# Score products of the first block's windowed attention: from three products on 64 rows to two on 128

## The chip, the cores and the metric

The kernel runs on one core of a Trainium2 chip. Its time is the device time of one execution in microseconds (us). Five engines work side by side: TensorE (PE in the profile, its weight loads PEld), VectorE (DVE), ScalarE (ACT), GpSimd (POOL) and SyncE (SP), which here issues nearly all DMAs. Each engine executes its own instructions in the order in which they stand.

## The reference

Two transformer blocks run over 512 tokens of 1024 features, all in float32. The change concerns the scores of the first block's windowed attention: 16 query heads of 64 features, four key heads (each for four query heads), query blocks of 128 tokens, each against the keys of its own block and of the two neighbours.

```python
def windowed_gqa_sink(q, k, v, sink):
    ...
    s = jnp.einsum('bnqgrd,bnkgd->bngrqk', qb, kw).astype(jnp.float32) * (d ** -0.5) + bias[None]
    sink_f = sink.astype(jnp.float32).reshape(1, 1, kvh, r, 1, 1)
    m = jnp.maximum(jnp.max(s, axis=-1, keepdims=True), sink_f)
    p = jnp.exp(s - m)
    denom = jnp.sum(p, axis=-1, keepdims=True) + jnp.exp(sink_f - m)
    o = jnp.einsum('bngrqk,bnkgd->bnqgrd', (p / denom).astype(v.dtype), vw)
```

The same normed input also feeds a state-space branch (SSD, eight groups) and two gates. After that come cross attention and a feed-forward part, and then the second block with its mixture of experts.

## The kernel before

**Precision.** TensorE multiplies operands of type fp32r, which hold fewer bits than float32. So every float32 operand of a dense product is split into a rounded part ("hi", or h) and the rest ("lo", or l), and a product becomes three: hi·hi, hi·lo and lo·hi (`mm3`, lines 275 to 279; the trace names lines 277, 278 and 279 for them). A weight unit of 128x1024 numbers is loaded by a DMA (`load_w`, line 266), rounded by ACT (`wh`, line 269) and completed by DVE (`wl`, line 272).

**Order of block 1** (`block1`). The input is normed, transposed and split into `hTh` and `hTl`. `attn_in` makes keys and values, `dt_section` the SSD's step sizes, `attention` the windowed attention, and `ssd` the SSD groups, with the gates (`gates1`) and the attention's output projection (`branch_a`) put among them. The program is written in this order. A scheduler in the tile framework then sets the order on each engine, by the dependencies and by its own estimates of durations, so that dense products of `ssd_in` and `gates1` (in the trace `mm<-hTh,wh` and the like) stand between the steps of the attention heads. No table in the kernel sets this.

**Keys.** `attn_in` projects 256 key features in two tiles of 128 rows, two key heads on top of each other. `kn` keeps each tile as it is and a second time with its halves swapped: one ACT copy of 128 rows (line 456), then two DMAs that move 64 rows each (lines 457 and 458). Four splits give `kh` and `kl`. Thus each key head lies once on rows 0 to 63 and once on rows 64 to 127.

**Queries.** Eight projections of 128 features give two query heads each, the first on rows 0 to 63, the second on rows 64 to 127. ACT writes the rounded part, scaled by 1/8, to `atH` (line 480), DVE the rest to `atL` (line 481), 128 rows at a time.

**Heads.** For each pair of heads, each head and each query block b, a score tile `sc` of 128 x L is made, where L is 256 for the first and the last block and 384 for the others. It is `mm3` with 64 rows of query and of key: the weights are the query block (64x128), the moving operand the keys (64xL). That makes 16 x 4 tiles and 192 products. DVE adds the alibi term and takes the maximum (line 508), and the four maxima of a head are negated (line 511). ACT exponentiates the sink's term (line 512) and each tile (line 515), and PE transposes the tile (`pt`, line 520). ACT or DVE copies it out (lines 523 and 525), and PE multiplies it with the values (`o`, line 528). After a pair of heads DVE divides (line 535), PE transposes the result (`ot`, line 540), and its split takes the place of the pair's queries in `atH` and `atL`. `sc`, `pt`, `o` and `ot` share three PSUM banks.

**What follows.** `ssd_p1` of a group works on four chunks. A chunk needs two broadcast loads `cs<-csd` (line 728), POOL's step matrices `D` (lines 696 and 698), a DVE chain (lines 732, 735 and 736) and then PE's products `yd` (line 741). `branch_a` begins when the last head's result is split: its products read `mm<-atH,wh` in the trace, and DVE closes each of its eight units with line 624 (`ta`).

Of the kernel before, what the change touches and what calls it, by code (L numbers as in the profile page):

```python
# [9 lines left out]
F32 = mybir.dt.float32  # L10
# [4 lines left out]
OP = mybir.AluOpType  # L15
# [11 lines left out]
def _units_b(w, cols):  # L27
    """Column blocks of 128 with all of K: [unit, partition, K tile, 128]."""
    K = w.shape[0]
    kt = K // 128  # L30
    return np.ascontiguousarray(
        np.stack([w[:, c].reshape(kt, 128, 128).transpose(1, 0, 2) for c in cols]))
# [6 lines left out]
def host_arrays(inp):  # L39
# [6 lines left out]
    def units_a(w, C=256, kt=4):  # L46
        """[column block, K half, partition, kt, C]"""
        K, N = w.shape
        return np.ascontiguousarray(
            w.reshape(K // (128 * kt), kt, 128, N // C, C).transpose(3, 0, 2, 1, 4))  # L50
# [117 lines left out]
class Emit:  # L168
# [30 lines left out]
    def psum(self, stack, n, mm, sa, sm):  # L199
        """the eight banks: dense products, two kinds of chains"""  # L200
# [30 lines left out]
    # ---------------------------------------------------------------- tools  # L231
# [49 lines left out]
    def proj_b(self, ps, units, act, halves=False):  # L281
        """feature-major: ps[128 cols, n tok]; units: list of W along K; act(k) -> (hi, lo)
        halves: the first half of the tokens as soon as it is there"""
# [19 lines left out]
    def proj_a(self, banks, units, act):  # L303
        """token-major: banks: psum tiles, two token tiles of 256 columns each; act(k, t) -> (hi, lo)"""
# [11 lines left out]
    def split(self, hi, lo, src, scale=None):  # L316
        """hi + lo = src * scale (scale: per-partition AP or None)"""
# [11 lines left out]
    def rstd(self, out, ss, n, eps=EPS):  # L329
        """out = (ss / n + eps) ** -0.5"""  # L330
# [5 lines left out]
    def rsqrt(self, v, eps, scale=1.0, tile=None):  # L336
        """(scale * v + eps) ** -0.5: a first guess from the bits, then Newton's iteration"""
# [13 lines left out]
    def norm_out(self):  # L351
        """where normed rows go, transposed and split: put(t, h, x) takes half a tile; hT(k) -> (hi, lo)"""
# [14 lines left out]
    def norm_T(self, gname):  # L367
        """rmsnorm of token-major tiles, transposed and split: step(t, x) takes a tile"""
# [80 lines left out]
    def attn_in(self):  # L449
        nc, a = self.nc, self.a  # L450
        # keys: natural and half-swapped, split
        kn = self.A("kn", (128, 2, 2, 512), F32)
        for m in range(2):
            ps = self.PM()
            self.proj_b(ps, [self.w0 if m == 0 else self.wb(8 + m)], self.hB, True)
            nc.scalar.copy(kn[:, 0, m, :], ps)
            nc.sync.dma_start(kn[0:64, 1, m, :], kn[64:128, 0, m, :])
            nc.sync.dma_start(kn[64:128, 1, m, :], kn[0:64, 0, m, :])
        self.kh = self.A("kh", (128, 2, 2, 512))
        self.kl = self.A("kl", (128, 2, 2, 512))  # L460
        for s in range(2):
            for m in range(2):
                self.split(self.kh[:, s, m, :], self.kl[:, s, m, :], kn[:, s, m, :])
# [7 lines left out]
    def attention(self):  # L471
        nc, a = self.nc, self.a
        # the result of a tile of queries takes the place of the queries
        self.atH = [self.A("atH") for _ in range(2)]
        self.atL = [self.A("atL") for _ in range(2)]
        for i in range(8):
            ps = self.PM()
            self.proj_b(ps, [self.wb(i)], self.hB)
            qh, ql = self.atH[i // 4][:, i % 4, :], self.atL[i // 4][:, i % 4, :]
            nc.scalar.activation(qh, ps, AF.Copy, scale=0.125)  # L480
            nc.vector.scalar_tensor_tensor(ql, ps, 0.125, qh.bitcast(F32), op0=OP.mult, op1=OP.subtract)
        for i in range(8):
            qh, ql = self.atH[i // 4][:, i % 4, :], self.atL[i // 4][:, i % 4, :]
# [4 lines left out]
            for hf in range(2):  # L488
# [3 lines left out]
                pr = slice(64 * hf, 64 * hf + 64)  # L492
                sw = 0 if hf == n % 2 else 1
                kh, kl = self.kh[pr, sw, n // 2, :], self.kl[pr, sw, n // 2, :]
# [5 lines left out]
                for b in range(4):  # L500
# [5 lines left out]
                    self.mm3(sc[:, :L], qh[pr, qs], ql[pr, qs], kh[:, k0:k1], kl[:, k0:k1], True, True)  # L506
# [95 lines left out]
    def gates1(self, f0, f1):  # L602
        """tanh of the halved gates, feature-major, to DRAM"""
# [10 lines left out]
    def branch_a(self):  # L614
        """(1 + tanh(ga / 2)) * (attn @ Wa), feature-major, to DRAM"""
# [11 lines left out]
    def conv(self, ps, ct, ntap, first, silu_scale=True):  # L627
        """half of the centred depthwise convolution of a psum tile, then 2 * half * sigmoid = silu"""
# [15 lines left out]
    def ssd_in(self, g):  # L644
        """projections of group g: B, C, x (feature-major, convolved) and the doubled silu of z (token-major)"""
# [18 lines left out]
    def ssd_p1(self, g, inp):  # L664
        """the part inside the chunks, and the chunks' states"""
# [4 lines left out]
        # token-major x and B  # L670
# [19 lines left out]
        # D[s, l]: the step of the forward direction for l >= s and that of the backward one for l <= s  # L690
# [10 lines left out]
        # per chunk: the part inside the chunk, and the chunk's states  # L701
# [5 lines left out]
        for c in range(4):  # L707
# [11 lines left out]
            # raw states into the slot that they feed: forward c + 1, backward c - 1  # L719
# [26 lines left out]
    def ssd_p2(self, g, st, yh, yl, j0):  # L746
        """the states' part, gate, norm, transposition"""
# [29 lines left out]
        # y carries a factor of 2 from the doubled silu: its mean square and the guard carry 4  # L777
# [4 lines left out]
    def ssd_p3(self, g, st, yh, yl, j0):  # L782
        """the normed rows, transposed"""
# [51 lines left out]
    def branch_b(self, p, yh, yl):  # L835
        """ssd @ Wb, a quarter of K at a time; the last quarter merges the branches"""
# [29 lines left out]
    def add_units(self, xs, src, nk, act, scale=1.0, last=True, then=None):  # L866
        """xs += scale * (act @ w), w as [column block, K part, ...] of 256 columns;
        last: the last columns go token tile by token tile; then(): the step that takes them"""
# [34 lines left out]
    def then(self, gname):  # L903
        """norm_T, begun when it is called; its results in nB"""
# [5 lines left out]
    def cross_mem(self):  # L910
        """the memory, normed and transposed"""
# [143 lines left out]
    def last_norm(self):  # L1055
        """the norm at the end of the first block and the first of the second: with s, q the mean squares of x and of x g,
        x <- x g (s + eps) ** -0.5, and of that the norm: x g (q + eps (s + eps)) ** -0.5 times its gain"""
# [1254 lines left out]
```

## Time and profile before

| what | value |
|---|---|
| time, three runs | 2176.49, 2178.56 (median), 2189.05 us |
| profiled execution | span 2182.1 us from the first to the last instruction |
| busy in the span | PE 93%, PEld 79%, DVE 62%, ACT 41%, POOL 23% |
| score products | first at 97.2 us, last at 287.9 us |

The profile gives no time of its own for that execution beside the span. Its span lies 3.5 us above the median of the three runs and within them. Times in rows count from the span's first instruction. A matmul's end is modelled, and successive matmuls overlap, so what a product costs PE in a stream is the distance from its start to the next start. "Granted clock" is a share of TensorE's full clock of 2.4 GHz; 0.50 is 1.2 GHz.

### The profile page before, as it was taken

The numbers are of one execution on the slowest core, as the hardware profiler recorded it, in microseconds if no ns is written. First come the engines' busy times: TensorE is split into PE (matmuls) and PEld (weight loads), VectorE is DVE, ScalarE is ACT, GpSimd is POOL, SyncE is SP. The second block draws the span as 40 slices with busy tenths as digits, with TensorE's granted clock in tenths as the row PEclk, the third lists the DMA queues.
The fourth block names the chain that finished last, engine by engine and source line by source line (L and its number), as shares of the span: only waits on it lengthen the run. The fifth ranks groups of instructions, "written<-read, shape, count | busy, mean of one in ns | idle before, by whom it ended". The sixth has DMA issues, their size and how long they took to land. (4 is left out here: it accounts for less than half of the span.)

```text
span 2182.1 us, 31237 instructions
## 1 busy us (share of the span) xinstructions
PE 2033.9 (93%) x11818; PEld 1730.2 (79%) x11818; DVE 1362.7 (62%) x2622; ACT 892.3 (41%) x1630; POOL 504.9 (23%) x515
## 2 busy tenths in 40 slices
PE   7999988989999988999999999899899999998995
PEld 7788877877787777888999999787878768886774
DVE  4566446786978765466334444667789452538885
ACT  4344434444545343254323222542232333246773
POOL 0000034034433142101111101503511110224444
PEclk9999999999999999999999999998899899998997
DMA  4211234323333254422222223224212104677976
GB/s 168 84 67 63 78 101 159 116 72 112 94 107 100 88 157 157 156 88 69 97 97 96 88 97 116 97 79 122 91 50 76 45 21 158 223 296 245 324 269 165
DMA packets 131302, 266.71 MB, mean 122 GB/s; under 512 B 22256, under 2 KB 67696, under 8 KB 127050
## 3 DMA queue, kind: packets, MB, share of 16 engines
q1 hardware_dynamic: 127690, 256.26, 35.5%
q0 software_dynamic: 3456, 8.39, 1.7%
q8 instruction: 95, 1.56, 0.3%
q14 instruction: 61, 0.50, 0.1%
HBM read 242.93 MB, written 25.35 MB: 123 GB/s over the span
## 5 line engine op out<-in xcount | busy, mean ns | idle before, releaser
L272 DVE TENSOR_TENSOR wl<-wr,wh 128x1024 fp32r<-128x1024 f32 (+1 forms) x272 | 316.4, 1164 | 288.9 <-ACT wh L269 277.9
L269 ACT CAST wh<-wr 128x1024 fp32r<-128x1024 f32 (+1 forms) x272 | 264.5, 973 | 548.5 <-PE mm L278 282.8
L279 PE MATMUL mm<-hTh,wl 128*128 128x512 f32 (+1 forms) x1056 | 412.4, 391 | 1.3 <-DVE wl L272 1.3
L277 PE MATMUL mm<-hTh,wh 128*128 128x512 f32 (+1 forms) x1056 | 411.9, 390 | 1.6 <-ACT hTh L320 0.9
L278 PE MATMUL mm<-hTl,wh 128*128 128x512 f32 (+1 forms) x1056 | 410.7, 389 | 0.8 <-DVE hTl L321 0.8
L279 PEld LDWEIGHTS mm<-hTh,wl 128*128 128x128 f32 x1056 | 203.4, 193 | 42.4 <-issue 5.1
L277 PEld LDWEIGHTS mm<-hTh,wh 128*128 128x128 f32 x1056 | 203.2, 193 | 39.6 <-issue 2.6
L278 PEld LDWEIGHTS mm<-hTl,wh 128*128 128x128 f32 x1056 | 203.2, 192 | 39.2 <-issue 3.2
L710 POOL TENSOR_TENSOR xw<-xt,dtT 128x256 f32<-128x256 f32 (+1 forms) x32 | 29.8, 932 | 551.4 <-ACT xt L678 551.4
L278 PE MATMUL mm<-wl,hTh 128*128 128x256 f32 x512 | 150.1, 293 | 0.0
L277 PE MATMUL mm<-wh,hTh 128*128 128x256 f32 x512 | 149.8, 293 | 0.0
L279 PE MATMUL mm<-wh,hTl 128*128 128x256 f32 x512 | 149.3, 292 | 0.0
L278 PE MATMUL mm<-wl,uh 128*128 128x256 f32 x512 | 145.0, 283 | 0.0
L279 PE MATMUL mm<-wh,ul 128*128 128x256 f32 x512 | 144.8, 283 | 0.0
L277 PE MATMUL mm<-wh,uh 128*128 128x256 f32 x512 | 144.7, 283 | 0.0
L876 DVE SCALAR_TENSOR_TENSOR x<-mm,x 128x256 f32<-128x256 f32 x152 | 57.5, 420 | 93.4 <-PE mm L279 92.8
L1042 POOL TENSOR_TENSOR ul<-r,uh 128x512 fp32r<-128x512 f32 x32 | 41.7, 1303 | 274.8 <-ACT uh L1041 274.8
L278 PEld LDWEIGHTS mm<-wl,hTh 128*128 128x128 f32 x512 | 100.9, 197 | 1.7 <-issue 0.7
L277 PEld LDWEIGHTS mm<-wh,hTh 128*128 128x128 f32 x512 | 100.8, 197 | 1.0 <-issue 0.2
L279 PEld LDWEIGHTS mm<-wh,hTl 128*128 128x128 f32 x512 | 100.8, 197 | 0.7 <-issue 0.5
L278 PEld LDWEIGHTS mm<-wl,uh 128*128 128x128 f32 x512 | 98.2, 192 | 0.5 <-DVE wl L272 0.2
L277 PEld LDWEIGHTS mm<-wh,uh 128*128 128x128 f32 x512 | 98.2, 192 | 0.3
(571 smaller groups left out, 4706.2 us busy)
## 6 DMA issues: line engine op xcount, KB each, us to landing
mr<-in_w_egu_dram SPq DMA_DIRECT2D x32, 1024.0 KB, 8.4
wr<-in_win_b_dram SPq DMA_DIRECT2D x59, 512.0 KB, 3.3
cs<-csd SPq DMA_DIRECT2D x64, 256.0 KB, 4.5
wr<-in_w_up_dram SPq DMA_DIRECT2D x32, 512.0 KB, 3.3
wr<-in_w_down_dram SPq DMA_DIRECT2D x32, 512.0 KB, 3.3
wr<-in_w_ed_dram SPq DMA_DIRECT2D x32, 512.0 KB, 4.5
wr<-in_w_b_dram SPq DMA_DIRECT2D x29, 512.0 KB, 3.3
wr<-in_win_a_dram SPq DMA_DIRECT2D x18, 512.0 KB, 3.3
```

Of the source, the lines that this page charges most:

```text
L269: nc.scalar.copy(w.hi, raw)
L272: e.tensor_tensor(w.lo, raw, w.hi.bitcast(F32), op=OP.subtract)
L277: mm(out, lh, rh, start=start, stop=False, skip_group_check=skip)
L278: mm(out, lh, rl, start=False, stop=False, skip_group_check=skip)
L279: mm(out, ll, rh, start=False, stop=stop, skip_group_check=skip)
L710: nc.gpsimd.tensor_tensor(xw[:, d0:d1], h3(xt[c])[:, None].to_broadcast([128, d1 - d0, 4, 64]), self.dtdec[:, c, d0:d1, H][:, :, :, None]. ...
L876: nc.vector.scalar_tensor_tensor(xv, ps[t // 2][:, (t % 2) * 256:(t % 2 + 1) * 256], scale, xv, op0=OP.mult, op1=OP.add)
L1042: nc.gpsimd.tensor_tensor(ul[:, j, :], r, uh[:, j, :].bitcast(F32), op=OP.subtract)
```

## The change

Each query head's rounded part and rest are stacked: head 0 of a pair has its rounded part on rows 0 to 63 and its rest on rows 64 to 127 of `atH`; head 1 has its rounded part on rows 64 to 127 and its rest on rows 0 to 63 of `atL`. For that ACT and DVE work on 64 rows at a time, and DVE writes to the other half of the rows from that which it reads. `kn` holds, for each key head, the same 64 features on both halves. A score tile is then the stack against `kh` plus the stack against `kl`, two products on 128 rows, which also contain the term lo·lo. The diff also takes out docstrings and comments, and later line numbers shift by two.

```diff
     def attn_in(self):
...
         kn = self.A("kn", (128, 2, 2, 512), F32)
+        h0, h1 = slice(0, 64), slice(64, 128)
         for m in range(2):
             ps = self.PM()
             self.proj_b(ps, [self.w0 if m == 0 else self.wb(8 + m)], self.hB, True)
-            nc.scalar.copy(kn[:, 0, m, :], ps)
-            nc.sync.dma_start(kn[0:64, 1, m, :], kn[64:128, 0, m, :])
-            nc.sync.dma_start(kn[64:128, 1, m, :], kn[0:64, 0, m, :])
+            for e, (own, other) in enumerate(((h0, h1), (h1, h0))):
+                nc.scalar.copy(kn[own, m, e, :], ps[own])
+                nc.sync.dma_start(kn[other, m, e, :], kn[own, m, e, :])
...
-        for s in range(2):
-            for m in range(2):
-                self.split(self.kh[:, s, m, :], self.kl[:, s, m, :], kn[:, s, m, :])
+        for m in range(2):
+            for e in range(2):
+                self.split(self.kh[:, m, e, :], self.kl[:, m, e, :], kn[:, m, e, :])
...
     def attention(self):
...
-            qh, ql = self.atH[i // 4][:, i % 4, :], self.atL[i // 4][:, i % 4, :]
-            nc.scalar.activation(qh, ps, AF.Copy, scale=0.125)
-            nc.vector.scalar_tensor_tensor(ql, ps, 0.125, qh.bitcast(F32), op0=OP.mult, op1=OP.subtract)
+            for q, own, other in ((self.atH, slice(0, 64), slice(64, 128)), (self.atL, slice(64, 128), slice(0, 64))):
+                q = q[i // 4][:, i % 4, :]
+                nc.scalar.activation(q[own], ps[own], AF.Copy, scale=0.125)
+                nc.vector.scalar_tensor_tensor(q[other], ps[own], 0.125, q[own].bitcast(F32), op0=OP.mult, op1=OP.subtract)
...
-                pr = slice(64 * hf, 64 * hf + 64)
-                sw = 0 if hf == n % 2 else 1
-                kh, kl = self.kh[pr, sw, n // 2, :], self.kl[pr, sw, n // 2, :]
+                q = (self.atL if hf else self.atH)[i // 4][:, i % 4, :]
+                kh, kl = self.kh[:, n // 2, n % 2, :], self.kl[:, n // 2, n % 2, :]
...
-                    self.mm3(sc[:, :L], qh[pr, qs], ql[pr, qs], kh[:, k0:k1], kl[:, k0:k1], True, True)
+                    nc.tensor.matmul(sc[:, :L], q[:, qs], kh[:, k0:k1], start=True, stop=False)
+                    nc.tensor.matmul(sc[:, :L], q[:, qs], kl[:, k0:k1], start=False, stop=True)
```

The scheduler also sets another order, from `dt_section` up to about the projections for the SSD's third group; from there on PE's order is that of before. Three places follow. The first is PE behind the second pair of heads (`ot` is that pair's result, `sc` the scores of the next head, `mm` dense products), before:

```order
653 L540 MATMUL ot<-consts,o 128x128 x4
654 L277 MATMUL sc<-kh,atH 128x256
655 L278 MATMUL sc<-kl,atH 128x256
656 L279 MATMUL sc<-kh,atL 128x256
657 L277 MATMUL sc<-kh,atH 128x384
658 L278 MATMUL sc<-kl,atH 128x384
659 L279 MATMUL sc<-kh,atL 128x384
660 L279 MATMUL mm<-wh,hTl 128x256
```

and now:

```order
652 L542 MATMUL ot<-consts,o 128x128 x4
653 L507 MATMUL sc<-kh,atH 128x256
654 L508 MATMUL sc<-kl,atH 128x256
655 L507 MATMUL sc<-kh,atH 128x384
656 L508 MATMUL sc<-kl,atH 128x384
657 L279 MATMUL mm<-wh,hTl 128x256
```

The third product of each tile is gone, and dense products stand around the score tiles as before. The second place is DVE in `dt_section`, among the first query splits (`dtx` is what PE's transposes wait for), before:

```order
31 L1153 RECIPROCAL dtu<-dtu 64x512
32 L481 SCALAR_TENSOR_TENSOR atL<-mm,atH 128x512
33 L1154 TENSOR_TENSOR dte<-dte,dtu 64x512
34 L272 TENSOR_TENSOR wl<-wr,wh 128x1024
35 L1155 TENSOR_TENSOR dtl<-dtl,dte 64x512
36 L1156 SCALAR_TENSOR_TENSOR dtx<-dtx,dtl 64x512
```

and now:

```order
31 L1155 RECIPROCAL dtu<-dtu 64x512
32 L484 SCALAR_TENSOR_TENSOR atH<-mm,atH 64x512
33 L1156 TENSOR_TENSOR dte<-dte,dtu 64x512
34 L272 TENSOR_TENSOR wl<-wr,wh 128x1024
35 L1157 TENSOR_TENSOR dtl<-dtl,dte 64x512
36 L484 SCALAR_TENSOR_TENSOR atL<-mm,atL 64x512
37 L1158 SCALAR_TENSOR_TENSOR dtx<-dtx,dtl 64x512
```

One query split more stands ahead of `dtx`. The third place is DVE in the first chunk of the SSD's first group, behind the last head (`cs` is the chain that PE's `yd` waits for, `ta` closes a unit of `branch_a`), before:

```order
332 L732 SCALAR_TENSOR_TENSOR cs<-cs,dtT 128x128 x4
333 L272 TENSOR_TENSOR wl<-wr,wh 128x1024
334 L735 TENSOR_TENSOR cs<-cs,CB 128x512
335 L736 TENSOR_TENSOR cs<-cs,D 128x512
336 L743 TENSOR_TENSOR y<-yd,sk 128x256
```

and now:

```order
345 L734 SCALAR_TENSOR_TENSOR cs<-cs,dtT 128x128 x4
346 L626 SCALAR_TENSOR_TENSOR ta<-ta,mm 128x512
347 L272 TENSOR_TENSOR wl<-wr,wh 128x1024
348 L737 TENSOR_TENSOR cs<-cs,CB 128x512
349 L738 TENSOR_TENSOR cs<-cs,D 128x512
350 L745 TENSOR_TENSOR y<-yd,sk 128x256
```

A unit of `branch_a` is closed inside the chain, because the dense products of the gates, which stood here before, are used up among the heads now: behind the last `ot` 49 of them were left before, and 1 is left now.

## Rows read from the trace of the kernel before

**Rows 1.** The page's part 1: busy time, share of the span, instructions
```profile
PE 2033.9 (93%) x11818; PEld 1730.2 (79%) x11818; DVE 1362.7 (62%) x2622; ACT 892.3 (41%) x1630; POOL 504.9 (23%) x515
```

**Rows 2.** Windows: busy us and instructions of each engine, granted clock, DMA
```profile
97.00:298.00 201.00, 200.99 (x1236) 168.73 (x1235) 115.63 (x278) 90.20 (x228) 0.00 (x0) 1.00 0.21 69
...
310.00:315.00 5.00, 0.89 (x4) 0.39 (x3) 4.90 (x5) 0.63 (x1) 4.92 (x5) 0.81 0.15 28
315.00:325.00 10.00, 8.45 (x27) 7.14 (x28) 4.73 (x10) 3.35 (x8) 6.32 (x7) 0.58 0.39 125
...
400.00:420.00 20.00, 19.97 (x115) 17.32 (x114) 16.90 (x24) 7.69 (x10) 0.00 (x0) 1.00 0.30 105
```

**Rows 3.** Tile sc: the third product, count, min/median/max ns, first and last start, forms
```profile
L279 PE MATMUL sc<-kh,atL x64: 274/307/342, 97.5 to 288.0; 64*128 64x256 f32 x32, 64*128 64x384 f32 x32
```

**Rows 4.** Timeline of PE around two score tiles: start, duration, instruction
```profile
186.28 0.39 PE L277 MATMUL mm<-hTh,wh 128*128 128x512 f32 x1
186.50 0.39 PE L278 MATMUL mm<-hTl,wh 128*128 128x512 f32 x1
186.82 0.44 PE L277 MATMUL sc<-kh,atH 64*128 64x384 f32 x1
187.10 0.33 PE L278 MATMUL sc<-kl,atH 64*128 64x384 f32 x1
187.28 0.33 PE L279 MATMUL sc<-kh,atL 64*128 64x384 f32 x1
187.45 0.28 PE L277 MATMUL sc<-kh,atH 64*128 64x256 f32 x1
187.57 0.28 PE L278 MATMUL sc<-kl,atH 64*128 64x256 f32 x1
187.69 0.28 PE L279 MATMUL sc<-kh,atL 64*128 64x256 f32 x1
187.89 0.50 PE L279 MATMUL mm<-hTh,wl 128*128 128x512 f32 x1
188.23 0.40 PE L277 MATMUL mm<-hTh,wh 128*128 128x512 f32 x1
188.47 0.39 PE L278 MATMUL mm<-hTl,wh 128*128 128x512 f32 x1
```

**Rows 5.** Timeline of PE: the first product of the first and of the last run
```profile
97.16 0.38 PE L277 MATMUL sc<-kh,atH 64*128 64x256 f32 x1
...
287.12 0.44 PE L277 MATMUL sc<-kh,atH 64*128 64x384 f32 x1
```

**Rows 6.** Tiles kn and atH: count, min/median/max ns, first and last start, forms
```profile
L456 ACT COPY kn<-mm x2: 582/585/588, 27.4 to 31.6; 128x512 f32<-128x512 f32 x2
...
L480 ACT ACTIVATE atH<-mm x8: 588/590/592, 54.8 to 98.0; 128x512 fp32r<-128x512 f32 x8
L481 DVE SCALAR_TENSOR_TENSOR atL<-mm,atH x8: 620/684/691, 56.6 to 99.4; 128x512 fp32r<-128x512 f32 x8
```

**Rows 7.** Timelines of DVE and of PE in dt_section
```profile
59.60 0.68 DVE L1156 SCALAR_TENSOR_TENSOR dtx<-dtx,dtl 64x512 f32<-64x512 f32 x1
...
60.34 0.27 PE L581 MATMUL p<-consts,dtx 64*128 64x64 f32 x1 [0.64 <-DVE dtx L1156]
```

**Rows 8.** Waits from 97 to 298 us: total us, times, longest
```profile
PEld o L528 <- ACT pT L523: 1.9, 9, 0.3
PEld sc L277 <- DVE m L508: 1.8, 5, 0.4
...
PEld o L528 <- DVE pT L525: 1.6, 7, 0.3
```

**Rows 9.** Waits of PE from 300 to 420 us: total us, times, longest
```profile
PE yd L741 <- DVE cs L736: 12.0, 5, 5.7
```

**Rows 10.** Timeline of PE behind the heads, and line L624 of DVE
```profile
316.56 1.94 PE L741 MATMUL yd<-xt,cs 128*128 128x64 f32 x8 [5.66 <-DVE cs L736]
318.25 0.77 PE L279 MATMUL mm<-hTh,wl 128*128 128x512 f32 x1
...
L624 DVE SCALAR_TENSOR_TENSOR ta<-ta,mm x8: 670/680/689, 328.2 to 390.6; 128x512 f32<-128x512 f32 x8
```

More of the change, by code (lines that the diff above doesn't have):

```diff
@@ L478, in attention @@
             self.proj_b(ps, [self.wb(i)], self.hB)
-            qh, ql = self.atH[i // 4][:, i % 4, :], self.atL[i // 4][:, i % 4, :]
-            nc.scalar.activation(qh, ps, AF.Copy, scale=0.125)
-            nc.vector.scalar_tensor_tensor(ql, ps, 0.125, qh.bitcast(F32), op0=OP.mult, op1=OP.subtract)
+            for q, own, other in ((self.atH, slice(0, 64), slice(64, 128)), (self.atL, slice(64, 128), slice(0, 64))):
+                q = q[i // 4][:, i % 4, :]
+                nc.scalar.activation(q[own], ps[own], AF.Copy, scale=0.125)
+                nc.vector.scalar_tensor_tensor(q[other], ps[own], 0.125, q[own].bitcast(F32), op0=OP.mult, op1=OP.subtract)
         for i in range(8):
-            qh, ql = self.atH[i // 4][:, i % 4, :], self.atL[i // 4][:, i % 4, :]
             n = i // 2
```

## Prediction, on record before the changed kernel ran

> **What bounds the kernel now.** I read the page's busy shares first, then windows over the stage that the change touches, then the timeline of PE inside that stage, and last the waits. The page shows PE busy for 93% of the span, far ahead of DVE [rows 1], so the question is whether PE also bounds the heads. From 97 to 298 us it is busy for 200.99 of 201 us at a granted clock of 1.00, while DVE is busy for 115.6 us and ACT for 90.2 us [rows 2]. Busy is not yet streaming, because ends of matmuls are modelled. So I looked at starts. Dense 512-column products follow each other every 0.22 to 0.24 us, and 384-column and 256-column score products every 0.17 to 0.18 and 0.12 us, but around each run of score products four distances are longer [rows 4]. The stage is bound by PE's stream and by those longer distances, and the weight loads of `o` and `sc` wait only 5.3 us in all for ACT and DVE [rows 8], hidden behind running products. Behind the heads it is different: from 310 to 315 us PE works 0.89 of 5 us, and the clock falls to 0.81 and then 0.58 [rows 2], because `yd` waits 5.66 us for DVE [rows 10]. From 300 to 420 us there are five such waits, 12.0 us together [rows 9].
>
> **The third product.** 64 products disappear, 32 of 256 columns and 32 of 384 [rows 3]. In the stream a 256-column one costs 0.12 us and a 384-column one 0.175 us, the mean of 0.18 and 0.17 [rows 4]: 32 x 0.12 + 32 x 0.175 = 3.8 + 5.6 = 9.4 us. The two that remain read 128 rows instead of 64. I take their cost as unchanged: the 128-row dense products show that PE sustains 512 columns in 0.23 us, the same 0.45 ns a column as the 0.175 us for 384 [rows 4].
>
> **The distances around a run.** With 0.23 us for a dense product, the last dense product before the run costs 0.32 us (186.50 to 186.82), 0.09 too much. The first score product costs 0.28 instead of 0.175, 0.105 too much. The last one costs 0.20 instead of 0.12, 0.08 too much, and the dense product behind it 0.34, 0.11 too much; the next is 0.01 late [rows 4]. That is 0.40 us for each run, whatever its length. In the timeline I count 40 runs of score products, the first from 97.16 and the last from 287.12 us [rows 5], so 40 x 0.40 = 16.0 us. A score product on 64 rows next to a dense one on 128 is what these places share, and afterwards no such neighbours are left. How much of the 16.0 us goes is not shown before: nothing of it, if the cost belongs to the score tiles and not to their rows, or all of it. I take all, because within a run and within the dense stream no distance is long, only where the two meet [rows 4].
>
> The Trainium skill, page "TensorEngine Tiling (Array Packing)", section "Key Properties", says that changing the tiling mode, and not just the tile, drains TensorE. By that rule the 40 changes into 64 rows and back are the cause and all 16.0 us go; without it only the 9.4 us would be sure. It gives no price; the rows do, 0.40 us for both changes of a run.
>
> Together 9.4 + 16.0 = 25.4 us come off PE's stream.
>
> **What is added on ACT and DVE.** The query parts take 16 ACT and 16 DVE instructions instead of 8 and 8. A DVE step of 64x512 takes 0.68 us [rows 7], as long as the query split of 128x512, 0.684 us [rows 6]; so halving the rows saves nothing, and 8 x 0.59 = 4.7 us of ACT and 8 x 0.68 = 5.5 us of DVE are added. Writing to the other half of the rows isn't shown in this trace. I take the same 0.68 us; half of it or twice would be the ends. A projection keeps PE busy for 24 x 0.23 = 5.5 us, and its splits (2 x 0.59 us of ACT, 2 x 0.68 us of DVE) fit beside it, so I cost them at nothing; with that cover gone they would cost up to 5.5 us. The exception is `dt_section`: PE already waits 0.64 us for `dtx` [rows 7], and one split more stands ahead of it. It costs 0.68 us, and two more dense products (0.46 us) now stand ahead of PE's wait, so 0.2 us are lost, 0 to 0.7 as bounds. The keys need four ACT copies instead of two, 2 x 0.585 us more [rows 6], still four DMAs, and the later splits wait for all of them. ACT's next weight cast stands behind that, but `kh` is first read at 97.16 us [rows 5], some 60 us later. I cost it at nothing, 1.2 us at most.
>
> **What the new order gives back among the heads.** Ahead of the last head's result 48 more dense products are spent, 48 x 0.23 = 11 us of work that merely moves. So the heads should shorten by 25.4 - 11 = 14 us, from 12.5 us (200 us for 16) to 11.6 us each. Within that time each head's chain (maximum on DVE, exponentials on ACT, transposes, copies) must still fit. Its weight loads already start as the producer ends [rows 8]. Where a run of score products lies between producer and consumer, PE arrives about 0.2 us earlier than now (half of the 0.40). At three such places in each of 16 heads that would be 9.6 us; with the added dense products as cover it can be 0. I take 2 us, near the low end, since all waits together in rows 8 are 5.3 us and hidden.
>
> **What it gives back behind the heads.** The first SSD chunk now has `ta`, 0.68 us [rows 10], inside the DVE chain that `yd` waits for, and in the second group the convolution steps of the next projections come forward among its chunks. The dense products between the first and the last `yd` of both groups stay about the same in number (291 before, 287 now, counted in the two orders). So the 12.0 us of waits remain and grow somewhat. Bounds: 4 us less, if one of the shorter waits closes, and 12 us more, if all double. I take 2.5 us, near the 0.68 us for each of four chunks.
>
> **The sum.** 25.4 - 0.2 - 2 - 2.5 = 20.7 us. Against the profiled execution that makes a span of 2182.1 - 20.7 = 2161.4 us. That span lies 3.5 us above the median of the three runs, and no other part of the execution is shown; from the median the time is 2178.6 - 20.7 = 2158 us. Everything after about 420 us stands in the same order and is fed by short prefetches, so an earlier start should carry to the end.
>
> **Rivals.**
> - *Nothing is given back.* The heads' added fillers cover each chain, and the SSD waits do not grow. PE's 19.97 busy of 20 us from 400 to 420 us [rows 2] speaks for a stage that takes in what comes; the just-in-time weight loads [rows 8] speak against. 2178.6 - 25.4 = 2153 us.
> - *The change doesn't free the switches.* If the long distances belong to score tiles and not to 64 rows, they stay, and there are 51 runs in the new order instead of 40: 9.4 - 11 x 0.40 = 5.0 us gained, 2174 us. That each run pays once, whatever its length, speaks against it.
> - *The chains take over.* The heads lose 9.6 us, or the SSD waits double (12 us): 2178.6 - 25.4 + 12 = 2165 us, and up to 2169 with part of both. For it: five `yd` waits already [rows 9]. Against: the new order puts about as many dense products behind each head's scores as before, and their times among the heads are covered today [rows 2].
> - *Slower: the SSD chunks stall as the first one does.* Place: `yd` in the two first groups. The first such wait costs 5.7 us and then work at the lower of the two clocks, 1.2 GHz for part of the time: from 315 to 325 us the mean is 0.58, so (1 - 0.58) x 8.45 busy us = 3.5 us, 9.2 us in all [rows 2, 10]. If DVE, loaded with the convolution steps, made four more of the eight chunks wait so, 36.8 us would be lost against 25.4 won: 2190 us. It decides from three such waits on. Against it: DVE is busy for only 4.73 of the 10 us from 315 to 325 [rows 2].
>
> **How the numbers follow.** The forecast, 2158 us, has a chance of 0.60; its own range is 2153 to 2164 (0 to 10 us given back). Nothing given back: 0.15. Switches stay: 0.07. Chains take over: 0.13. Slower: 0.05. The range from 2150 us (all 25.4 us and about 3 us less of `yd` waits) to 2172 us (most of the chains' case) leaves out about 2 in 10. About 1%, 21.8 us or a time under 2156.8, is what a measurement can tell from no change. Of the forecast's 0.60 about 0.24 lies there, and of the first rival 0.14: 0.38 for faster. Slower by over 1% needs more than 2200 us, 0.02 out of the last rival. The rest, 0.60, is within 1%.
>
> **What would show it.** Right: two products for each of 64 tiles on 128 rows; dense products beside them at 0.23 us, with no distance of 0.32 or 0.34; the last run of score products at about 275 us (12 us earlier) and about 20 us gained at 420 us and at the end. Wrong: a granted clock below 1.00 among the heads, weight loads that leave PE idle there for more than 5 us, `yd` waits of over 18 us in the two groups, query splits much longer than 0.68 us, or long distances that remain around score tiles.

## The result, and the profile after

The changed kernel takes 2161.78 us, the median of 8 runs (2152.91 to 2170.14). The kernel before, run beside it on the same chip, takes 2183.94 us (8 runs, 2171.73 to 2189.05). The ratio is 0.9899, with a 95% interval from 0.9872 to 0.9926: about 22 us or 1.0% less, and the interval reaches to both sides of 1%. The forecast was 20.7 us less, 2158 us. Its 2158 stood on the median of three runs of the kernel before, 2178.56 us; the eight runs lie 5.4 us higher, so the differences are what can be compared.

The page's part 1 of the kernel after, beside [rows 1]: PE has 64 instructions less, DVE 8 and ACT 10 more.

```profile
PE 2000.5 (93%) x11754; PEld 1711.1 (80%) x11754; DVE 1367.0 (64%) x2630; ACT 898.7 (42%) x1640; POOL 503.8 (23%) x515
```

**The score products.** The tile view of `sc` in the kernel after: line, engine, operation, count, shortest/median/longest ns, first and last start, forms. Each of the 64 tiles is made by two products, on 128 rows.

```profile
L507 PE MATMUL sc<-kh,atH x32: 274/338/446, 98.3 to 266.1; 128*128 128x256 f32 x16, 128*128 128x384 f32 x16
L508 PE MATMUL sc<-kl,atH x32: 278/308/340, 98.4 to 266.2; 128*128 128x256 f32 x16, 128*128 128x384 f32 x16
L507 PE MATMUL sc<-kh,atL x32: 277/339/423, 108.9 to 277.8; 128*128 128x256 f32 x16, 128*128 128x384 f32 x16
```

The timeline of PE around two score tiles after (start, duration, instruction) is the place to lay beside [rows 4]. Go by the distances between starts.

```profile
229.71 0.39 PE L279 MATMUL mm<-hTh,wl 128*128 128x512 f32 x1
229.93 0.33 PE L507 MATMUL sc<-kh,atL 128*128 128x384 f32 x1
230.10 0.34 PE L508 MATMUL sc<-kl,atL 128*128 128x384 f32 x1
230.28 0.40 PE L277 MATMUL mm<-hTh,wh 128*128 128x512 f32 x1
230.51 0.28 PE L507 MATMUL sc<-kh,atL 128*128 128x256 f32 x1
230.63 0.27 PE L508 MATMUL sc<-kl,atL 128*128 128x256 f32 x1
230.74 0.40 PE L278 MATMUL mm<-hTl,wh 128*128 128x512 f32 x1
230.97 0.39 PE L279 MATMUL mm<-hTh,wl 128*128 128x512 f32 x1
231.21 0.39 PE L277 MATMUL mm<-hTh,wh 128*128 128x512 f32 x1
```

They are 0.22, 0.17, 0.18, 0.23, 0.12, 0.11, 0.23, 0.24 us. A dense product ahead of a score product takes 0.22 or 0.23 us where it took 0.32, and the one behind it 0.23 where it took 0.34. None of the four long distances is left here. The same holds through the heads: a dense product directly behind a score product takes 0.33 to 0.34 us in all of 27 places before, and 0.23 to 0.24 in all of 36 after.

The weight loads, which the prediction did not look into, show where the distance arises. The timeline of PEld before, at the places of [rows 4]:

```profile
186.28 0.19 PEld L278 LDWEIGHTS mm<-hTl,wh 128*128 128x128 f32 x1
186.82 0.18 PEld L277 LDWEIGHTS sc<-kh,atH 64*128 64x128 f32 x1 [0.35 <-issue]
...
187.89 0.19 PEld L279 LDWEIGHTS mm<-hTh,wl 128*128 128x128 f32 x1
```

And after, the load for the score product at 229.93:

```profile
229.71 0.19 PEld L507 LDWEIGHTS sc<-kh,atL 128*128 128x128 f32 x1
```

The load for the dense product at 186.50 starts 0.22 us ahead of it, together with the product before. The loads for the first score product (186.82) and for the dense product behind the run (187.89) start together with their own products. In the heads of the kernel before, dense and score products change between 64 and 128 rows at 54 places: there no load starts more than 0.002 us ahead of its product, while at the 568 places where the rows stay it starts at least 0.11 us ahead. A load takes 0.18 to 0.19 us. Two of them that are not hidden come to 0.37 us, close to the 0.40 of a run. After, the loads run ahead again. Why a load is not taken ahead where the rows change, these rows do not show.

**How far the program has got.** Ends of two profiles are poor places to compare here (below, on the clock). So I take three marks on PE, counted from its first transpose `tr`: the first transpose of the first SSD group (`xt`), with which the heads' stretch ends, and the first `yt`, behind which the program is again in the order of before. In the tile view the next fence has the first starts of the kernel before, and the one behind it those of the kernel after.

```profile
L360 PE MATMUL tr<-consts,xn x128: 270/273/477, 8.1 to 1402.6; 128*128 128x128 f32 x128
...
L676 PE MATMUL xt<-consts,cv x64: 272/273/279, 297.7 to 765.8; 128*128 128x128 f32 x64
...
L794 PE MATMUL yt<-consts,y x64: 270/273/476, 425.9 to 849.5; 128*128 128x128 f32 x64
```

```profile
L360 PE MATMUL tr<-consts,xn x128: 270/273/476, 9.0 to 1378.6; 128*128 128x128 f32 x128
...
L678 PE MATMUL xt<-consts,cv x64: 272/273/281, 287.0 to 740.8; 128*128 128x128 f32 x64
...
L796 PE MATMUL yt<-consts,y x64: 270/273/475, 402.3 to 825.8; 128*128 128x128 f32 x64
```

From `tr` to `xt`: 289.6 us before, 278.0 after, 11.6 less. From `xt` to `yt`: 128.2 before, 115.3 after, 12.9 less. Nothing of the 11.6 arises ahead of the heads: from the first score product to `xt` it is 200.5 us before and 188.7 after, 11.8 less. Together 24.5 us are gained at the first `yt`, and the last `tr`, at some 1400 us, still shows 24.9 (1394.5 against 1369.6). What was won stays won, as the prediction said of everything behind 420 us.

**The splits and `dt_section`.** The tile view of `atH` after (columns as above). These rows answer to [rows 6]; the second one reads the bank's rows 64 to 127 and writes rows 0 to 63.

```profile
L483 ACT ACTIVATE atH<-mm x8: 577/592/593, 55.2 to 99.3; 64x512 fp32r<-64x512 f32 x8
L484 DVE SCALAR_TENSOR_TENSOR atH<-mm,atH x8: 683/684/685, 57.2 to 100.3; 64x512 fp32r<-64x512 f32 x8
```

Half the rows cost as much as all (684 ns), and writing to the other half costs nothing on top: in the kernel with the splits alone (below), where nothing crosses, the same step takes 688 ns. In `dt_section`, in the timeline of PE, the wait of [rows 7] is now 1.20 us instead of 0.64:

```profile
61.79 0.27 PE L583 MATMUL p<-consts,dtx 64*128 64x64 f32 x1 [1.20 <-DVE dtx L1158]
```

**Behind the heads.** The waits of PE in the kernel after, from 280 to 420 us (total us, times, longest), answer to [rows 9]:

```profile
PE yd L743 <- DVE cs L738: 13.4, 4, 7.2
```

The wait became 1.4 us longer in sum and is now met four times, the first for 7.19 us [rows 10: 5.66]. Yet this stretch came out shorter than forecast. Windows say why (columns as in [rows 2]): first the stretch from `xt` to `yt` before, then the three pieces of it in which the clock is at the lower level.

```profile
298.00:426.00 128.00, 115.98 (x570) 96.60 (x569) 85.43 (x162) 50.08 (x101) 44.33 (x42) 0.93 0.43 138
...
313.10:323.30 10.20, 6.75 (x20) 5.74 (x21) 4.83 (x5) 2.72 (x7) 8.14 (x8) 0.50 0.34 103
367.70:371.10 3.40, 3.40 (x13) 2.84 (x12) 0.42 (x1) 0.00 (x0) 3.32 (x4) 0.50 0.61 192
381.30:384.70 3.40, 3.40 (x12) 2.85 (x12) 1.94 (x4) 0.65 (x2) 0.01 (x1) 0.51 0.52 158
```

After: the heads, the stretch from `xt` to `yt`, and its one piece at the lower level.

```profile
97.00:298.00 201.00, 200.99 (x1281) 176.15 (x1280) 119.55 (x285) 99.84 (x245) 8.98 (x9) 1.00 0.27 89
...
287.00:402.00 115.00, 101.54 (x521) 84.78 (x520) 82.26 (x160) 47.40 (x97) 43.31 (x42) 0.96 0.44 136
...
302.70:312.90 10.20, 6.47 (x19) 5.54 (x20) 4.90 (x8) 0.65 (x2) 7.53 (x7) 0.50 0.58 180
```

From `xt` to `yt` PE has 49 instructions less (570 and 521), 48 of them the dense products that moved among the heads. Its busy time falls by 14.4 us and its idle time rises from 12.0 to 13.5. Of the 14.4 us the 48 products at 0.23 us are 11.0. The clock gives most of the rest: at the lower level PE is busy for 13.6 us before and for 6.5 after, and the upper level would do the same in half of the time, so by this estimate the low clock costs 6.8 us before and 3.2 after, 3.6 less. In the repeated pair of profiles (below) it is 8.2 and 4.8, 3.4 less. Both kernels have such a piece around the first long wait; the pieces behind it, from 367 us before, are gone in this profile after.

### The profile page after: what moved, and what is told of

It is laid out like the page before. It is cut to its first block, busy times and chain, and to the rows that moved or that the text cites. A ratio compares the mean times of both kernels' runs of the same rounds, so it can differ in the third digit from the quotient of the medians.

```text
span 2152.2 us, 31122 instructions
## 1 busy us (share of the span) xinstructions
PE 2000.5 (93%) x11754; PEld 1711.1 (80%) x11754; DVE 1367.0 (64%) x2630; ACT 898.7 (42%) x1640; POOL 503.8 (23%) x515
```

## The experiments

Five questions were open. Do the long distances come from the 64 rows or from the score tiles? How much of the gain is the removed product? What do the added splits cost? Does the gain repeat? Is there a second place of the kind? The median times of several kernels below stand beside the runs of before on the same chip, and the distances `tr` to `yt` come from the profiles (before: 417.8 us).

**The two kernels again, one execution each.**

> The kernel before, unchanged but for a docstring, profiled once more, to see how far two profiles of one kernel differ. Theory (the first block repeats, and what differs between profiles comes from lower clocks in the second block): first transpose of the SSD's rows (yt) within 1.5 us of the earlier profile, counted from the first transpose of all; differences of up to 12 us behind 1480 us. Rival (the first block varies as much): more than 4 us of difference at that point.

> The changed kernel, unchanged but for a docstring, profiled once more. Theory: the first transpose of the SSD's rows again 23 to 26 us earlier than before, counted from the first transpose of all. Rival (the 24.5 us of the first profile had luck in the SSD chunks): less than 20 us.

Measured: before 2175.87 us and after 2161.01 us. `tr` to `yt`: 419.4 us before (9.8 to 429.2) and 394.1 us after (8.2 to 402.3), 25.3 less, as against 24.5 in the first pair. From `tr` to `xt` it is 289.5 and 277.7. So up to the first `yt` these profiles of one kernel agree within 1.6 us (1.5 expected). A third profile of the kernel after (taken for the second place, below) does not: it has 399.3 us from `tr` to `yt`, 6.0 more than the first. Its window says why:

```profile
68.00:78.20 10.20, 10.20 (x34) 8.66 (x33) 4.88 (x9) 3.22 (x6) 0.00 (x0) 0.50 0.31 86
```

Ahead of the heads, where the other profiles have the upper level, it has 10.2 us at the lower one, which by the same estimate costs 5.1 us; its first score product comes 94.5 us behind `tr` instead of 89.3. This piece stands behind the wait for `dtx` (1.2 us in all three profiles of the kernel after); whether that wait, longer than before, has to do with it is not shown. Counted from the first score product to the first `yt`, the three profiles have 304.0, 305.1 and 304.8 us, and the two of before 328.7 and 330.5. Times at the end differ too: counted from `tr`, this pair is 13.3 us apart at the end of its spans (2174.1 and 2159.2 us) and the first pair 30.9 (2182.1 and 2152.2). That is taken up under the clock.

**Two products on 64 rows.** The kernel before without its third product, the low part of the queries times the high part of the keys (line 506).

```diff
-  self.mm3(sc[:, :L], qh[pr, qs], ql[pr, qs], kh[:, k0:k1], kl[:, k0:k1], True, True)
+  nc.tensor.matmul(sc[:, :L], qh[pr, qs], kh[:, k0:k1], start=True, stop=False)
+  nc.tensor.matmul(sc[:, :L], qh[pr, qs], kl[:, k0:k1], start=False, stop=True)
```

> The kernel before with the product of the queries' rest and kh left out (two products on 64 rows for a score tile; the output lacks that term). Theory (each run of 64-row products costs 0.40 us beside its columns): 9.4 us of products gone, but 54 runs in its order instead of 40, so 5.6 us more of switches: 2 to 4 us faster than before, distances of 0.32 and 0.34 us still there. Rival (fewer products and the new order are the gain, the rows don't matter): as fast as the changed kernel, some 22 us faster than before.

Measured: 2169.53 us (4 runs) against 2186.19 (23 runs), ratio 0.992 (0.9897 to 0.9943), 12 to 23 us less. That is far more than the 2 to 4 us expected, and the time alone would let the rival's 22 us stand, so it matters where the time went. The timeline of PE, around a tile of which only two products are left:

```profile
124.54 0.40 PE L278 MATMUL mm<-hTl,wh 128*128 128x512 f32 x1
124.87 0.44 PE L506 MATMUL sc<-kh,atH 64*128 64x384 f32 x1
125.15 0.34 PE L507 MATMUL sc<-kl,atH 64*128 64x384 f32 x1
125.42 0.49 PE L279 MATMUL mm<-hTh,wl 128*128 128x512 f32 x1
```

And its marks in the tile view:

```profile
L360 PE MATMUL tr<-consts,xn x128: 270/273/477, 9.8 to 1399.0; 128*128 128x128 f32 x128
...
L795 PE MATMUL yt<-consts,y x64: 271/273/474, 422.6 to 845.8; 128*128 128x128 f32 x64
```

The distances are still long: 0.33 us into the tile, 0.28 for its first product, 0.27 for its last, where 0.175 would be the stream. There are more runs, 54 in place of 40 counted in the two timelines. At the first `yt` 5.0 us are gained (412.8), and 5.3 at the last `tr`, 1400 us. That is near the 9.4 us of the products less the 14 x 0.40 = 5.6 us of new runs, and far from the 24.5 of the kernel after. The other 12 us of its profile come behind 1400 us, where nothing was changed: from the last `tr` to the end it takes 767.8 us, the first profile of before 779.5, but the second one of before 766.8 (the clock, below). All four of its runs lie at 2168 to 2172 us; why the four are as short as the profiled one is not explained.

**Three products on 128 rows.** The kernel after with its second product issued twice. It has the third product's work, without 64-row products.

```diff
   nc.tensor.matmul(sc[:, :L], q[:, qs], kh[:, k0:k1], start=True, stop=False)
+  nc.tensor.matmul(sc[:, :L], q[:, qs], kl[:, k0:k1], start=False, stop=False)
   nc.tensor.matmul(sc[:, :L], q[:, qs], kl[:, k0:k1], start=False, stop=True)
```

> The changed kernel with its second product made twice (three products on 128 rows; the output counts the term with kl twice). Theory: the 9.4 us of products are back, the switches stay away: about 12 to 14 us faster than before. Rival (fewer products are the gain): as slow as before, within 3 us.

Measured: 2170.43 us (8 runs) against 2186.19, ratio 0.9937 (0.991 to 0.9964), 13.8 us less by the ratio (8 to 20), as expected. Its marks in the tile view:

```profile
L360 PE MATMUL tr<-consts,xn x128: 270/273/477, 8.5 to 1388.7; 128*128 128x128 f32 x128
...
L797 PE MATMUL yt<-consts,y x64: 271/273/473, 411.2 to 835.8; 128*128 128x128 f32 x64
```

`tr` to `yt` is 402.7 us, 15.1 less than before: with all of the products still there, the change's larger part is already had. The kernel after is 9.4 us shorter again (402.7 and 393.3). From the first score product it is 8.2 to 9.3 us with the three profiles of the kernel after, so the third product comes at about its price in the stream.

**The third of them on 64 rows.** The same kernel, with PE's instructions in the same order, but the added product reads rows 0 to 63 alone.

```diff
-  nc.tensor.matmul(sc[:, :L], q[:, qs], kl[:, k0:k1], start=False, stop=True)
+  nc.tensor.matmul(sc[:, :L], q[0:64, qs], kl[0:64, k0:k1], start=False, stop=True)
```

> As the run with three products on 128 rows, but the third one on rows 0 to 63 alone, with as many columns (its output adds half of that term once more). The only difference is 64 rows in one product of each of 64 tiles. Theory: every tile now switches to 64 rows and back, 64 x 0.40 = 25.6 us more than with three on 128 rows, so 10 to 14 us slower than before. Rival (rows don't matter): the same time as three on 128 rows.

Measured: 2192.83 us (10 runs) against 2186.19, ratio 1.0021 (1.0 to 1.0041). In time it is 0 to 9 us slower than before, less than the 10 to 14 expected, and slower than the kernel with three products on 128 rows by 22 us (medians). The timeline of PE at two of its tiles:

```profile
125.86 0.36 PE L507 MATMUL sc<-kh,atH 128*128 128x256 f32 x1
126.06 0.28 PE L508 MATMUL sc<-kl,atH 128*128 128x256 f32 x1
126.27 0.38 PE L509 MATMUL sc<-kl,atH 64*128 64x256 f32 x1
126.58 0.44 PE L507 MATMUL sc<-kh,atH 128*128 128x384 f32 x1
126.86 0.33 PE L508 MATMUL sc<-kl,atH 128*128 128x384 f32 x1
```

Here all is of one tile of scores, and no product of another stage stands between. Still the product ahead of the 64-row one takes 0.21 us in place of 0.12, and the 64-row one 0.31. The first product of the next tile, back on 128 rows, takes 0.28 where 384 columns take 0.175. (The 0.20 us of the very first one, behind `ot`, are the same in the kernel with three products on 128 rows.) These are the extras of [rows 4], now where 64 rows meet 128 within a tile. The weight loads fit: at all of its 127 such changes between score and dense products no load starts more than 0.003 us ahead of its product. The marks:

```profile
L360 PE MATMUL tr<-consts,xn x128: 270/273/477, 7.7 to 1411.4; 128*128 128x128 f32 x128
...
L797 PE MATMUL yt<-consts,y x64: 271/273/473, 433.6 to 858.5; 128*128 128x128 f32 x64
```

`tr` to `yt` is 425.9 us, 23.2 more than with 128 rows: 0.36 us for each of 64 tiles (0.40 expected), in one line that differs by its rows alone. All of it arises in the heads; from `xt` to `yt` the two kernels differ by 0.1 us. The rival that the distances belong to score tiles falls with this, since the tiles and their neighbours are the same in both.

**The splits alone.** The kernel before, with the copies of the keys and the splits of the queries in two halves of 64 rows each.

```diff
-  nc.scalar.copy(kn[:, 0, m, :], ps)
+  nc.scalar.copy(kn[0:64, 0, m, :], ps[0:64])
+  nc.scalar.copy(kn[64:128, 0, m, :], ps[64:128])
...
-  nc.scalar.activation(qh, ps, AF.Copy, scale=0.125)
-  nc.vector.scalar_tensor_tensor(ql, ps, 0.125, qh.bitcast(F32), op0=OP.mult, op1=OP.subtract)
+  for r in (slice(0, 64), slice(64, 128)):
+      nc.scalar.activation(qh[r], ps[r], AF.Copy, scale=0.125)
+      nc.vector.scalar_tensor_tensor(ql[r], ps[r], 0.125, qh[r].bitcast(F32), op0=OP.mult, op1=OP.subtract)
```

> The kernel before with the key copies and the query splits made in halves of 64 rows (2 more ACT copies, 8 more ACT and 8 more DVE splits, nothing crossing halves), the same output. Theory: hidden beside PE's projections, within 1 us of before at the first head's scores and at the end. Rival: ACT and DVE are on the path there, up to 5.5 us slower.

Measured: 2183.08 us (10 runs) against 2186.19, ratio 0.9994 (0.9971 to 1.0018), no difference. Its marks:

```profile
L360 PE MATMUL tr<-consts,xn x128: 270/273/476, 8.1 to 1402.7; 128*128 128x128 f32 x128
...
L796 PE MATMUL yt<-consts,y x64: 270/273/475, 425.5 to 849.8; 128*128 128x128 f32 x64
```

417.4 us against 417.8, and the first score product comes 0.4 us later (89.5 us behind `tr`, before 89.1): the 11 us of added ACT and DVE work are hidden.

**The marks side by side.** Microseconds between first starts, from the tile views; the fourth column is PE's busy time at the lower level of the clock from `xt` to `yt`, the last one the time from the last `tr` to the end of the span.

| profile | `tr` to `sc` | `sc` to `xt` | `xt` to `yt` | busy at the lower level | last `tr` to end |
|---|---|---|---|---|---|
| before | 89.1 | 200.5 | 128.2 | 13.6 | 779.5 |
| before, again | 88.9 | 200.6 | 129.9 | 16.3 | 766.8 |
| splits alone | 89.5 | 201.9 | 126.0 | 14.8 | 767.7 |
| two products on 64 rows | 88.2 | 208.0 | 116.6 | 8.0 | 767.8 |
| three products on 128 rows | 89.4 | 189.1 | 124.2 | 9.2 | 779.7 |
| the third of them on 64 rows | 89.2 | 212.6 | 124.1 | 10.2 | 779.9 |
| after | 89.3 | 188.7 | 115.3 | 6.5 | 773.6 |
| after, again | 89.0 | 188.7 | 116.4 | 9.6 | 779.7 |
| after, third profile | 94.5 | 188.6 | 116.2 | 9.1 | 778.1 |

From `sc` to `xt`, where the clock is at 1.00 in all of them, profiles of one kernel agree within 0.1 us.

**A second place of the kind.** In the second block's attention the scores `lg` are one product on 64 rows per head and query block, among products on 128. In the trace of the kernel after, 37 runs of 64-row products lie between the first and the last `lg`, 29 of them with `lg`; with the edit 15 are left. On top of the kernel after, its keys are held twice, the other head's half filled with zeros, so that the product can read 128 rows.

```diff
-  self.kd = [self.G("kd") for _ in range(2)]
+  self.kd = [[self.G("kd"), self.cp.tile([128, 512], F32, name=f"ke{n}")] for n in range(2)]
+  for n in range(2):
+      for u in range(2):
+          nc.gpsimd.memset(self.kd[n][u][hs[1 - u]], 0.0)
...
-  nc.scalar.copy(self.kd[n], ps[n])
+  for u in range(2):
+      nc.scalar.copy(self.kd[n][u][hs[u]], ps[n][hs[u]])
...
-  nc.tensor.matmul(ps[:, :L], self.bqT[R, h // 2, ts], self.kd[h // 4][R, :L], start=True, stop=True)
+  nc.tensor.matmul(ps[:, :L], self.bqT[:, h // 2, ts], self.kd[h // 4][h % 2][:, :L], start=True, stop=True)
```

> The changed kernel, and in the second block's attention the scores (lg) also on 128 rows: both heads' queries against keys with zeros on the other head's rows, as many products as before, the same result. Runs of 64-row products there fall from 45 to 15 in PE's order. Theory: 30 x 0.40 = 12 us less if PE's stream bounds that stage, 6 to 12 us with its waits for DVE, so some 28 to 34 us faster than the kernel before. Rival (that stage is bound by ACT's and DVE's chain): no gain over the changed kernel, about 22 us faster than before.

Measured: 2148.55 us (5 runs) against 2178.76 (9 runs), ratio 0.9858 (0.9832 to 0.9884), some 30 us less, as expected. To set it against the kernel after rather than the one before, both were run on one chip:

> The changed kernel once more, timed beside the one that also has the second block's scores on 128 rows. Theory: about 22 us faster than before (ratio 0.990).

> The changed kernel with the second block's scores (lg) on 128 rows against zero-filled keys, timed beside the changed kernel on one chip. Theory (30 runs fewer, and the stretch from the first lg to the router's bank is 4 us shorter in the trace): 4 to 8 us faster than the changed kernel. Rival (the earlier difference was the clock's luck in the second block): within 2 us of it.

Measured: the kernel after 2157.74 us (6 runs), ratio 0.9909 (0.9876 to 0.9942); with `lg` on 128 rows 2155.09 us (6 runs), ratio 0.9888 (0.986 to 0.9915), both against 2176.4 us (11 runs). The two differ by 2.6 us and their intervals overlap: less than the 4 to 8 us expected, and the times don't tell whether it gains. In the traces the way from the first `lg` to the router's first product `rb<-tk,oh` takes 298.8 us in both profiles with the edit, and 301.5, 303.0 and 307.3 us in three of the kernel after. In this stretch PE is busy at the lower clock for 6.8 us in both profiles with the edit, and for 3.4, 6.8 and 17.1 us in the three. Like against like, 298.8 against 303.0, it gains some 4 us there. It beats the kernel before in both comparisons; that it beats the kernel after in time stays open.

## Why the prediction was right, and the step that was off

**The third product** (forecast 9.4 us) measures 9.4 us in one pair of profiles: the difference between three and two products on 128 rows at the first `yt`. With the other profiles of the kernel after, counted from the first score product, it is 8.2 and 8.5, so the agreement to a tenth is luck, and the size is not. The price in the stream was the right one to use. Multiplying 64 by the 307 ns that [rows 3] give as a median duration would have made it 19.6 us.

**The distances** (forecast 16.0 us) were put down to the meeting of 64 and 128 rows, with all of them going. Both hold. They are gone from the timeline after, and they stay in the kernel with two products on 64 rows. They come back inside the score tiles when one product in three reads 64 rows, at 0.36 us for each tile (forecast 0.40 a run). The kernel with three products on 128 rows gains 15.1 us, 11.4 of them among the heads (200.5 to 189.1). That the rows are the cause is shown; what in TensorE makes it so is shown only as far as the weight loads go, which are not taken ahead where the rows change. The Trainium skill, page "TensorEngine Tiling (Array Packing)", section "Key Properties", has it that a change of the tiling mode drains TensorE. The runs agree in that each change costs time, 0.36 to 0.40 us for going to 64 rows and coming back; a drain as such is not seen in the trace.

**The added splits** (forecast nothing) cost nothing that the kernel with them alone could show, and writing to the other half of the rows takes 684 ns, the value taken. In `dt_section` the wait rose by 0.56 us although two more dense products stand ahead of it: more than the 0.2 us forecast, within its bounds of 0 to 0.7. At the first score product 0.2 and 0.1 us of it are left (89.3 against 89.1 us behind `tr`, 89.0 against 88.9 in the repeated pair).

**The heads** should give back 2 us, and the stretch up to `xt` shorten by 25.4 - 11 - 0.2 - 2 = 12.2 us. It is 11.6 us, and 11.8 in the repeated pair. From the first score product it is 11.8 in the first pair, where 25.4 - 11 would make 14.4, so 2.6 us were given back (forecast 2). PE is busy through the heads, at a clock of 1.00, as before. How the 2.6 us divide is not shown: 40 runs at 0.36 instead of 0.40 us would be 1.6, and the weight loads of `pt` and `o` wait 6.2 us for ACT and DVE where they waited 4.0, the mechanism that the prediction named.

**Behind the heads** is the term that was off. Forecast was 2.5 us given back, from the longer wait of the first chunk and from the convolution steps among the later ones: 11 - 2.5 = 8.5 us less from `xt` to `yt`. Measured are 12.9, and 13.5 in the repeated pair. The wait did lengthen, by 1.4 us in sum, instead of 2.5; it is met four times and not five. What the forecast lacked is the clock, a term that it put at nothing: PE's work at the lower level fell from 13.6 to 6.5 us, worth 3.6 us by the estimate above, and 3.4 in the repeated pair. So 11.0 - 1.4 + 3.6 = 13.2 us stand against the 12.9 measured, and 2 us were won there where 2.5 were to be lost. I had priced the stretch by DVE's chain alone and had not asked what the clock would do in the 100 us behind a wait, although [rows 2] showed it at 0.58 for 10 of them. That fewer waits are the reason for the better clock is plausible and not shown.

In sum the profiles show 24.5 and 25.3 us up to 420 us, against 20.7 forecast. The rival "nothing is given back" (25.4) is nearer in them. The median time, 22.2 us less, lies between the two, and its interval of 16 to 28 us holds both. So the forecast's nearness to the median, 1.5 us, is in part luck: the 4.4 us missed behind the heads lie inside that interval. "The switches stay" (5.0) and "the SSD chunks stall" (12 us lost) are excluded by the ratio's interval; "the chains take over" (9 to 13 us gained) is too.

## What to carry to other kernels

A product that reads 64 rows among products that read 128 costs more than its columns: here 0.36 to 0.40 us for going over and back, more than the 0.175 us of the product itself, as the weight loads at both changes (0.18 to 0.19 us each) are not hidden. Look at distances between starts, not at busy time, which read 200.99 of 201 us both before and after; and where an operand has a high and a low part of 64 rows, stack them along the contraction, which also saves a product. When work moves ahead of a stage that waits, count the clock behind the wait as well as the wait, and read a small gain between two marks that enclose the stretch whose order differs.

## What had not been expected: two levels of the clock in unchanged work

Behind 1400 us nothing was changed in any kernel but those with the `lg` edit, and yet profiles differ there by up to 13 us: from the last `tr` to the end they take 767 to 768 us in three profiles and 778 to 780 in five, with 774 in the first one after. The kernel with the splits alone is 0.4 us ahead of before at the first `yt`, and 11.7 us at the end of its span (spans of 2170.4 and 2182.1 us, `tr` at 8.1 in both). Windows (columns as in [rows 2]) at nearly the same places in the work, first of before, then with the splits alone, then after:

```profile
1505.00:1523.00 18.00, 16.52 (x87) 15.09 (x88) 11.35 (x27) 1.89 (x3) 12.08 (x16) 0.58 0.37 100
1720.00:1738.00 18.00, 18.00 (x64) 12.99 (x63) 7.05 (x23) 3.71 (x12) 1.23 (x2) 0.54 0.19 59
```

```profile
1505.00:1523.00 18.00, 13.61 (x97) 12.14 (x98) 15.42 (x33) 2.45 (x4) 12.90 (x16) 0.87 0.43 109
1720.00:1738.00 18.00, 17.15 (x111) 13.12 (x109) 8.88 (x28) 4.61 (x14) 4.79 (x7) 1.00 0.03 4
```

```profile
1481.00:1499.00 18.00, 16.53 (x87) 15.05 (x88) 11.29 (x27) 1.89 (x3) 12.00 (x16) 0.57 0.43 99
1696.00:1714.00 18.00, 17.92 (x108) 13.81 (x107) 9.25 (x31) 5.52 (x18) 1.23 (x2) 0.92 0.21 59
```

In 18 us from 1720 us PE gets through 64 instructions at a clock of 0.54, busy all of the time, and through 111 at 1.00. That is the lower level, 1.2 GHz, for most of the window against the upper, 2.4 GHz. The two windows don't hold quite the same products. The kernel before has both windows low, the one with the splits both high or nearly so (0.87 and 1.00), and the kernel after one of each. The kernel with two products on 64 rows, which gained 12 us behind 1400 us, has both high too (0.88 and 1.00). The times of a single kernel vary alike: of the runs of before, one with a mean clock of 0.972 took 2171.93 us, and one with 0.963 took 2182.20, on one chip. What decides which level an execution gets was not found. For a change worth 1% it means that one pair of times can be off by half of the effect (13.3 and 30.9 us at the end of two pairs of profiles, 25.3 and 24.5 at 420 us, but 18.5 with the third profile after, whose clock was low ahead of the heads). Several runs are needed, or marks that leave such stretches out.
